# Seven-product pairs for two of four row parts of the feed-forward down projections

## The chip, the core and the metric

The kernel runs on one core of a Trainium2 chip. The time is the device time of one execution in microseconds; several executions are timed and their median is given. One further execution was recorded by the hardware profiler, and all rows of the trace come from it.

## What is computed

The reference is one inference step of a decoder trunk with two layers (DEPTH 2), D_MODEL 1024, 512 prompt tokens and 8 x 4 sample tokens, so 544 token columns in all. Each layer is a half-step feed-forward, a block of three mixers merged by gates, a second half-step feed-forward, and a gated input embedding. Everything is fp32. What the change touches is the feed-forward, with D_FF 2816:

```python
def swiglu(h, w_up, w_down):
    gate, up = jnp.split(h @ w_up, 2, axis=-1)
    return (jax.nn.silu(gate) * up) @ w_down
...
    h = rmsnorm(x, w['g_ffn1'])
    x = x + 0.5 * swiglu(h, w['w_ffn1_up'], w['w_ffn1_down'])
...
    h = rmsnorm(x, w['g_ffn2'])
    x = x + 0.5 * swiglu(h, w['w_ffn2_up'], w['w_ffn2_down'])
```

## The kernel before

Activations lie with channels on the partitions and the 544 tokens on the free axis. Every fp32 value is split into a high part in fp32r (ScalarE copies it) and a low part (VectorE subtracts), and a product is three matmuls: low x high, high x high, high x low.

**Two forms of product.** A plain product (`mm3`, L313) has a 128x128 weight block and runs over 544 columns as two halves of 272, so six matmuls. The seven-product form (`s_pair`, matmuls on L337) takes a pair of output tiles, pairs of input tiles and the two halves of the tokens as a 2x2 by 2x2 block product and does it in seven block products instead of eight, after Winograd. For it the weights W11, W12, W21, W22 are combined into R1 to R4 and the inputs into a *set* per pair of input tiles: B11, B21, B22 and the sums T1 to T4, each of 272 columns with a high and a low part. It keeps four half banks of PSUM, X, Y, Z and V. After the first product ScalarE copies X to Z (L636), after the third it copies X out and VectorE writes V = Y - copy (L640, L641), after the fifth there is one more such pair (L645, L646); the fourth product goes on in Z, the sixth in V, and the third, fifth and seventh in X.

**Weights.** A *unit* is 512 columns of weights: four blocks of a plain product, or the four sets' blocks for one of the seven products. `unit` brings a unit to its end `AHEAD` = 4 units before it is used, in stages: SP loads it (`load`, L234 to L241; for R1 and R2 a POOL DMA adds a second block to what has landed, L242), VectorE adds R3 and R4 (`split_add`, L248), ScalarE makes the high part (`split_hi`, L255), VectorE the low part (`split_lo`, L260). The sums stand two units ahead of the low parts and the loads `LOADS` = 9 units ahead of the sums. All weights and most temporaries live in a pool of 85 slots of 128 x 544; a slot that is given back goes to the end of the queue of free ones, and what is written into it next waits for its last reader.

**A feed-forward.** `ffn` goes over the 22 row tiles of the hidden layer in four row parts of 4, 6, 6 and 6 (`FF_PARTS`). For each tile `ff_group` does the gate and the up projection as one pair, 84 matmuls, whose results are scaled by the norm (L711, L714), put through Silu (L663), multiplied (L666) and split (L669, L672). These closing steps wait in `self.later`: `tick` runs behind each unit, and the step with number n comes n ticks after the pair. The down projection of a part is four pairs of outputs (`down`), all plain in the kernel before: 72 matmuls for six row tiles, 48 for four, and two updates of the residual x (L728). They stand in a queue `todo` and are placed between the pairs of the next part; those of the last part follow at the end. There are four feed-forwards. In each the first tile's projections are plain (four tiles in the first feed-forward).

**Mixing.** `mix` uses seven-product pairs on full sets made by `s_inputs(gain, True)`, for the projections w_in and the gates; plain products there use other operands. TensorE, VectorE, ScalarE, SP and POOL each work through their own instructions in program order.

Of the kernel before, what the change touches and what calls it, by code (L numbers as in the profile page):

```python
# [24 lines left out]
NFF = DFF // P  # L25
FF_PARTS = (4, 6, 6, 6)
NPLE = 2
G = 4
# [9 lines left out]
NSLOT = 85  # L38
LOADS = 9
USE_MERGE = 57  # L40
AHEAD = 4
MAX_AHEAD = 24
# [32 lines left out]
def _places(seq):  # L75
    places = []
    off = 0
    for i, (kind, spec) in enumerate(seq):
        if kind == "P" or spec[0] == 0:
            u0 = i  # L80
            at, off = off, off + P * UC * (1 if kind == "P" else 4)
        places.append((at, u0))
    assert off == N_WEIGHTS
    return places
# [22 lines left out]
class Kern:  # L107
# [99 lines left out]
    def weight(self, u):  # L207
        kind, spec = self.seq[u]
        return (PRODUCTS[spec[0]][0] if kind == "S" else ""), *self.places[u]

    def new_raw(self, w, u0, readers):
        t = self.alloc(F32)
        self.raw[w, u0] = [t, readers]
        return t[0][:, :UC]

    def read_raw(self, w, u0):
        return self.raw[w, u0][0][0][:, :UC]

# [7 lines left out]
    def load(self, u):  # L226
        w, at, u0 = self.weight(u)
        dma = self.nc.sync.dma_start

        def src(i=0, n=1):  # L230
            return self.ins["wts"][at:at + P * UC * n].rearrange("(p c) -> p c", c=UC * n)[:, i * UC:(i + 1) * UC]
# [20 lines left out]
    def split_hi(self, u):  # L252
        w, _, u0 = self.weight(u)
        self.ops[u] = a, b = self.alloc(F32R), self.alloc(F32R)
        self.nc.scalar.activation(a[0][:, :UC], self.read_raw(w, u0), AF.Copy)  # L255

    def split_lo(self, u):
        w, _, u0 = self.weight(u)
        hi, lo = (t[0][:, :UC] for t in self.ops[u])
        self.nc.vector.tensor_sub(lo, self.read_raw(w, u0), hi.bitcast(F32))  # L260
        self.done_raw(w, u0)
# [8 lines left out]
    def unit(self, entry):  # L270
        self.u += 1
        if self.keep:
            self.used += 2
        if self.dry:
            self.seq.append(entry)
            self.use.append(self.used)
            return NULL, NULL
        self.release(self.held)
        to = self.u + AHEAD
        for v in range(self.n_st[3], self.n_st[3] + (self.extra if entry[0] == "P" else 0)):  # L280
            if to < v <= self.u + MAX_AHEAD and self.fits(v + 1):
# [6 lines left out]
        return tuple(t[0][:, :UC] for t in pair)  # L288

# [48 lines left out]

    def s_unit(self, i, name, l, m1, m2):
        assert self.left == 0  # L340
        return self.unit(("S", (i, name, l, m1, m2)))

# [76 lines left out]
    def s_inputs(self, gain, full):  # L419
# [5 lines left out]
        def steps(q):  # L425
# [17 lines left out]
            def hi_b():  # L443
# [13 lines left out]
                tiles.append((b[0][:, :], b[1][:, :]))  # L457
                for src, hi, lo, g in st["b"]:
# [22 lines left out]
            def hi_t():  # L481
                A, B = st["e"][0][0], st["t"][0]
                c = own(*self.rpair())
                if full:
                    d = own(*self.rpair())
                    t1, t4 = ((d[0][:, h], d[1][:, h]) for h in (h1, h2))
                    st["h"] = ((A[:, :], d[0][:, :], d[1][:, :]), (B[:, :], c[0][:, :], c[1][:, :]))
                else:
                    a, d = st["a"], own(self.slot(F32R))
                    t1, t4 = (a[0][:, h2], a[1][:, h2]), (d[0][:, h1], d[1][:, h2])  # L490
                    st["h"] = ((A[:, h1], *t1), (B[:, :], c[0][:, :], c[1][:, :]), (A[:, h2], *t4))
                for src, hi, lo in st["h"]:
                    nc.scalar.activation(hi, src, AF.Copy)  # L493
                sets[q].update(T1=t1, T2=(c[0][:, h1], c[1][:, h1]), T3=(c[0][:, h2], c[1][:, h2]), T4=t4)
# [123 lines left out]

    def s_pair(self, name, l, m1, m2, sets, s1, s2, out):
        nc = self.nc  # L620
        h1, h2 = slice(0, HT), slice(HT, T)
        a, b = s1[0], s2[0]
        banks = [self.ring_bank() for _ in range(4)]
# [4 lines left out]
        for i, (w, x) in enumerate(PRODUCTS):  # L628
            bk = bank[w]
            wt = self.s_unit(i, name, l, m1, m2)  # L630
            new = w in ("W21", "R2")
            for q, xs in enumerate(sets):
                self.mm_s(bk, wt, xs[x], q, new and q == 0, q == len(sets) - 1, not new)
            if w == "W21":
                self.touch(banks[2], sets[0]["B11"][0])
                nc.scalar.activation(Z, X, AF.Copy)  # L636
            elif w == "R2":
                self.touch(banks[3], sets[0]["B11"][0])
            elif w == "R3":
                nc.scalar.activation(a[:, h2], X, AF.Copy)  # L640
                nc.vector.tensor_sub(V, Y, a[:, h2])  # L641
            elif w == "W22":
                out(b, h1, Z)
            elif w == "R1":
                nc.scalar.activation(b[:, h2], X, AF.Copy)  # L645
                nc.vector.tensor_sub(a[:, h2], Y, b[:, h2])  # L646
            elif w == "W12":
                out(a, h1, V)
            elif w == "R4":
                out(b, h2, X)  # L650
            self.tick()

    def ff_group(self, up, l, j, inp, first, plain, hs, hsl):
        nc = self.nc
        t_, o_ = self.slot(), self.slot()
        t, o = t_[0], o_[0]
        a, b = self.rpair()
        hi, lo = a[0][:, :], b[0][:, :]
        hs.append((hi, lo))
        hsl.extend((a, b))  # L660

# [16 lines left out]
        def dr():  # L678
            nc.vector.tensor_mul(o[:, :], o[:, :], self.rstd[:, :])

        if plain > 0:
# [20 lines left out]
            elif plain > 1:  # L702
                fin = (e0, e1, dz, None, d1, d2, d3)
            else:
# [3 lines left out]
        else:  # L708
            r = self.rstd
            self.s_pair(up, l, NFF + j, j, inp.sets, o_, t_,  # L710
                        lambda to, h, ps: nc.vector.tensor_mul(to[:, h], ps, r[:, h]))  # L711

            def dr2():
                nc.vector.tensor_mul(o[:, HT:], o[:, HT:], r[:, HT:])  # L714

            fin = (dz, dr2, d1, d2, d3)
        self.later += [(1 + i, f) for i, f in enumerate(fin) if f]

    def ffn(self, l, which, inp, nxt, tail=None):
        nc = self.nc  # L720
        up, dn = f"w_ffn{which}_up", f"w_ffn{which}_down"
        plain = N_PLAIN if self.start else 1

        def down(m, hs, hsl, j0, last=False):
# [12 lines left out]
        j0 = 0  # L737
        for n in FF_PARTS:
            hs, hsl = [], []
            items = len(todo)  # L740
            for i in range(n):
                j = j0 + i
                self.extra = EXTRA[0] if j < plain else EXTRA[7]
                if j == plain:
                    self.drop(*inp.zs)
                self.ff_group(up, l, j, inp, j == 0, plain - j, hs, hsl)
                while len(todo) > items * (n - 1 - i) // n:
# [38 lines left out]
    def mix(self, l, inp, nxt):  # L786
# [4 lines left out]
        full = self.s_inputs(inp.gain, True)  # L791
        sets, xr, sl = full.sets, full.tiles, full.sl
        steps = self.skew(full.fs, 0, 3) + self.skew(full.fs, 3, 6)
# [4 lines left out]
        def pair(z1, z2, f=None):  # L798
            s1, s2 = self.slot(), self.slot()
            self.s_pair("w_in", l, z1, z2, sets, s1, s2,  # L800
                        lambda to, h, ps: nc.scalar.activation(to[:, h], ps, f or AF.Copy))  # L801
            if f:
# [514 lines left out]
def _layout(inputs, seq):  # L1317
# [9 lines left out]
    for kind, spec in seq:  # L1327
        if kind == "P":
            part = [block(*s) for s in spec]
        elif spec[0] == 0:  # L1330
            _, name, l, m1, m2 = spec
            part = [block(name, l, 2 * q + i, m) for m in (m1, m2) for i in range(2) for q in range(KD // 2)]
        else:
            continue
# [61 lines left out]
```

## Time and profile before

| what | before |
|---|---|
| median of 3 runs | 2403.72 us (2402.2 to 2403.86) |
| profiled execution | 2402.33 us |
| its span, first to last instruction | 2400.6 us |
| TensorE busy | 2386.3 us |
| VectorE busy | 1776.0 us |
| ScalarE busy | 1234.2 us |
| DMA, mean | 137 GB/s |
| mean granted clock of TensorE | 0.999 |

Busy time is the time in which at least one instruction of the engine runs. Matmuls are pipelined and overlap, so that a mean record of 288 ns doesn't mean 288 ns per matmul: the distance between starts is what counts, and it comes from the chain of waits. The profiled execution's own time is 1.7 us longer than its span.

### The profile page before, as it was taken

The numbers are of one execution on the slowest core, as the hardware profiler recorded it, in microseconds if no ns is written. First come the engines' busy times: TensorE is split into PE (matmuls) and PEld (weight loads), VectorE is DVE, ScalarE is ACT, GpSimd is POOL, SyncE is SP. The second block draws the span as 40 slices with busy tenths as digits, with TensorE's granted clock in tenths as the row PEclk, the third lists the DMA queues.
The fourth block names the chain that finished last, engine by engine and source line by source line (L and its number), as shares of the span: only waits on it lengthen the run. The fifth ranks groups of instructions, "written<-read, shape, count | busy, mean of one in ns | idle before, by whom it ended". The sixth has DMA issues, their size and how long they took to land.

```text
span 2400.6 us, 47687 instructions
## 1 busy us (share of the span) xinstructions
PE 2386.3 (99%) x18777; PEld 2371.8 (99%) x18777; DVE 1776.0 (74%) x3212; ACT 1234.2 (51%) x2421; POOL 225.8 (9%) x277
## 2 busy tenths in 40 slices
PE   9999999999999999999999999999999999999998
PEld 9999999999999999999999999999999999999998
DVE  8776667877878777667777766778778777766685
ACT  7544444755565544445554444556556555544463
POOL 1101000111100110100010110001111011101000
PEclk9999999999999999999999999999999999999999
DMA  6655561766554555655165555516555545556431
GB/s 212 143 147 143 145 171 36 178 150 151 149 141 119 145 146 145 150 134 166 55 151 134 144 157 128 167 56 171 146 152 152 150 102 149 152 131 154 128 107 38
DMA packets 180033, 329.76 MB, mean 137 GB/s; under 512 B 20256, under 2 KB 22560, under 8 KB 179808
## 3 DMA queue, kind: packets, MB, share of 16 engines
q1 hardware_dynamic: 141264, 255.92, 34.8%
q0 software_dynamic: 36672, 68.51, 16.9%
q8 instruction: 147, 2.41, 0.4%
q10 hardware_dynamic: 1872, 2.29, 0.3%
q14 instruction: 78, 0.64, 0.1%
HBM read 323.64 MB, written 2.99 MB: 136 GB/s over the span
## 4 chain that ended last, share of the span: by engine, by line
PE 92%; DVE 4%; ACT 3%; issue 0%; DMA 0%; DVEq 0%; ACTq 0%; SPq 0%
PE ps L337 54%; PE ps L313 33%; PE ps L904 2%; PE ps L1170 2%; ACT s L459 1%; DVE s L260 1%; DVE s L498 1%; ACT s L437 1%; DVE acc L400 0%; PE ps L1053 0%; DVE s L469 0%; ACT s L493 0%; ACT s L255 0%; ACT s L399 0%; DVE s L476 0%
## 5 line engine op out<-in xcount | busy, mean ns | idle before, releaser
L337 PE MATMUL ps<-s,s 128*128 128x272 f32 x10332 | 1311.9, 288 | 2.2 <-DVE s L695 2.2
L337 PEld LDWEIGHTS ps<-s,s 128*128 128x128 f32 x10332 | 1302.3, 188 | 3.4 <-DVE s L695 2.8
L313 PE MATMUL ps<-s,s 128*128 128x272 f32 x7536 | 958.9, 288 | 1.3 <-ACT s L459 1.3
L313 PEld LDWEIGHTS ps<-s,s 128*128 128x128 f32 x7536 | 949.8, 188 | 1.6 <-ACT s L459 1.5
L260 DVE TENSOR_TENSOR s<-s,s 128x512 fp32r<-128x512 f32 x1211 | 810.1, 685 | 34.3 <-ACT s L255 32.2
L255 ACT ACTIVATE s<-s 128x512 fp32r<-128x512 f32 x1211 | 710.3, 623 | 188.3 <-DVE s L248 180.3
L242 POOL DMA_DIRECT2D s<-in_wts x246 | 211.0, 872 | 1936.4 <-DMA s<-in_wts 567.3
L636 ACT ACTIVATE ps<-ps 128x272 f32<-128x272 f32 x123 | 47.1, 383 | 493.7 <-PE ps L337 440.1
L728 DVE SCALAR_TENSOR_TENSOR x<-ps,x 128x544 f32<-128x544 f32 x128 | 92.6, 724 | 214.1 <-PE ps L313 213.7
L248 DVE TENSOR_TENSOR s<-s,s 128x512 f32<-128x512 f32 x246 | 168.6, 685 | 0.0
L641 DVE TENSOR_TENSOR ps<-ps,s 128x272 f32<-128x272 f32 x123 | 55.2, 449 | 120.3 <-ACT s L640 119.9
L711 DVE TENSOR_TENSOR s<-ps,rstd 128x272 f32<-128x272 f32 x243 | 106.2, 437 | 11.5 <-PE ps L337 9.9
L640 ACT ACTIVATE s<-ps 128x272 f32<-128x272 f32 x123 | 48.9, 398 | 102.3 <-PE ps L337 101.9
L646 DVE TENSOR_TENSOR s<-ps,s 128x272 f32<-128x272 f32 x123 | 54.3, 441 | 60.1 <-ACT s L645 58.9
L645 ACT ACTIVATE s<-ps 128x272 f32<-128x272 f32 x123 | 48.6, 395 | 66.6 <-PE ps L337 66.4
L801 ACT ACTIVATE s<-ps 128x272 f32<-128x272 f32 x126 | 49.9, 396 | 52.0 <-PE ps L337 51.6
L946 DVE TENSOR_TENSOR s<-ps,s 128x544 f32<-128x544 f32 x48 | 34.8, 725 | 54.6 <-PE ps L313 54.5
L669 ACT ACTIVATE s<-s 128x544 fp32r<-128x544 f32 x88 | 57.9, 658 | 29.0 <-DVE s L666 29.0
L672 DVE TENSOR_TENSOR s<-s,s 128x544 fp32r<-128x544 f32 x88 | 63.3, 720 | 3.6 <-ACT s L669 3.6
L666 DVE TENSOR_TENSOR s<-s,s 128x544 f32<-128x544 f32 x88 | 63.2, 718 | 1.5 <-ACT s L663 1.5
L663 ACT ACTIVATE s<-s 128x544 f32<-128x544 f32 x88 | 57.2, 651 | 11.4 <-DVE s L711 9.7
L1170 PE MATMUL ps<-s,s 128*128 128x256 f32 (+1 forms) x480 | 60.7, 288 | 0.0
(155 smaller groups left out, 1036.7 us busy)
## 6 DMA issues: line engine op xcount, KB each, us to landing
s<-in_wts SPq DMA_DIRECT2D x965, 256.0 KB, 3.3
s<-in_wts POOLq DMA_DIRECT2D x246, 256.0 KB, 5.0
x<-in_xT SPq DMA_DIRECT2D x4, 272.0 KB, 4.5
x<-in_xT ACTq DMA_DIRECT2D x4, 272.0 KB, 5.0
s<-in_pT POOLq DMA_DIRECT2D x4, 272.0 KB, 4.3
out_yT<-s SPq DMA_DIRECT2D x4, 144.0 KB, 1.9
out_yT<-s ACTq DMA_DIRECT2D x4, 144.0 KB, 1.9
s<-in_st_in POOLq DMA_DIRECT2D x2, 272.0 KB, 3.0
```

The costliest lines, as they stand in the source:

```text
L242: self.nc.gpsimd.dma_start(out=t, in_=src(1 if w == "R1" else 2, 4), accum_op=ALU.add)
L248: self.nc.vector.tensor_add(self.new_raw(w, u0, 2 if w == "R3" else 1), self.read_raw(a, u0), self.read_raw(b, u0))
L255: self.nc.scalar.activation(a[0][:, :UC], self.read_raw(w, u0), AF.Copy)
L260: self.nc.vector.tensor_sub(lo, self.read_raw(w, u0), hi.bitcast(F32))
L313: self.nc.tensor.matmul(ps[:, h, :HT], a, bh, start=first and i == 0, stop=last and i == 2)
L337: self.nc.tensor.matmul(ps, a, b, start=first and i == 0, stop=last and i == 2, skip_group_check=go_on)
L666: nc.vector.tensor_mul(o[:, :], o[:, :], t[:, :])
L669: nc.scalar.activation(hi, o[:, :], AF.Copy)
L672: nc.vector.tensor_sub(lo, o[:, :], hi.bitcast(F32))
L711: lambda to, h, ps: nc.vector.tensor_mul(to[:, h], ps, r[:, h]))
L728: nc.vector.scalar_tensor_tensor(xm, self.pv(pst[i]), 0.5, xm, op0=ALU.mult, op1=ALU.add)
L1170: nc.tensor.matmul(ps, a, b[:, c], start=first and i == 0, stop=last and i == 2)
```

## The change

The down projections of row parts 1 and 2 of every feed-forward (`FF_S`) run as seven-product pairs (`down_fast`), three sets for six row tiles, so that a unit of their weights has 384 columns instead of 512. The sets are made in `ff_group` out of two gated tiles: the steps e1 (even tile) and e2 and t (odd tile) take the place of the plain split d2 and d3. The pair's results go to x in quarter steps of 272 columns. The four pairs of such a part run two behind the first and two behind the second gate pair of the next part (`DRAIN`). `unit`'s loads are 7 instead of 9 units ahead of the sums, the low parts 5 instead of 4 ahead of the use. In the mixing sets the second half of the first tile's split is no longer made (nothing reads it), and T1 takes its place, so that a set has seven slots instead of eight. In the first feed-forward the closing steps from d1 on come some ticks later.

```diff
+DRAIN = 2, 2, 0, 0, 0, 0
+FF_S = (False, True, True, False)
...
-LOADS = 9
+LOADS = 7
...
-AHEAD = 4
+AHEAD = 5
...
+    def width(self, u):
+        kind, spec = self.seq[u]
+        return UC if kind == "P" else P * spec[-1]
...
                 if full:
-                    st["b"] = [(E1[:, :], a[0][:, :], a[1][:, :], g1)]
-                    tiles.append((a[0][:, :], a[1][:, :]))
+                    st["b"] = [(E1[:, h1], a[0][:, h1], a[1][:, h1], g1)]
...
-                if full:
-                    d = own(*self.rpair())
-                    t1, t4 = ((d[0][:, h], d[1][:, h]) for h in (h1, h2))
-                    st["h"] = ((A[:, :], d[0][:, :], d[1][:, :]), (B[:, :], c[0][:, :], c[1][:, :]))
-                else:
-                    a, d = st["a"], own(self.slot(F32R))
-                    t1, t4 = (a[0][:, h2], a[1][:, h2]), (d[0][:, h1], d[1][:, h2])
-                    st["h"] = ((A[:, h1], *t1), (B[:, :], c[0][:, :], c[1][:, :]), (A[:, h2], *t4))
+                a, d = st["a"], own(self.slot(F32R))
+                t1, t4 = (a[0][:, h2], a[1][:, h2]), (d[0][:, h1], d[1][:, h2])
+                st["h"] = ((A[:, h1], *t1), (B[:, :], c[0][:, :], c[1][:, :]), (A[:, h2], *t4))
...
+        def e1_hi():
+            self.drop(t_)
+            st.update(a=self.rpair(), o=o_)
+            hsl.extend(st["a"])
+            nc.scalar.activation(st["a"][0][0][:, h1], o[:, h1], AF.Copy)
+
+        def e1_lo():
+            a = [p[0] for p in st["a"]]
+            nc.vector.tensor_sub(a[1][:, h1], o[:, h1], a[0][:, h1].bitcast(F32))
+
+        def e2_hi():
+            st["b"] = self.rpair()
+            hsl.extend(st["b"])
+            nc.scalar.activation(st["b"][0][0][:, :], o[:, :], AF.Copy)
+            A, B = st["o"][0], t
+            nc.vector.tensor_sub(B[:, h2], A[:, h2], o[:, h2])
+            nc.vector.tensor_sub(B[:, h1], B[:, h2], A[:, h1])
+
+        def e2_lo():
+            b, A, B = [p[0] for p in st["b"]], st["o"][0], t
+            nc.vector.tensor_sub(A[:, h1], A[:, h1], A[:, h2])
+            nc.vector.tensor_add(A[:, h2], o[:, h1], B[:, h1])
+            nc.vector.tensor_sub(b[1][:, :], o[:, :], b[0][:, :].bitcast(F32))
+            self.drop(o_)
+
+        def t_hi():
+            c, d = self.rpair(), self.slot(F32R)
+            hsl.extend((*c, d))
+            A, B = st["o"][0], t
+            a, b, c, d = *([p[0] for p in st[k]] for k in "ab"), [p[0] for p in c], d[0]
+            st["h"] = ((A[:, h1], a[0][:, h2], a[1][:, h2]), (B[:, :], c[0][:, :], c[1][:, :]), (A[:, h2], d[:, h1], d[:, h2]))
+            for src, hi, _ in st["h"]:
+                nc.scalar.activation(hi, src, AF.Copy)
...
+        def t_lo():
+            for src, hi, lo in st["h"]:
+                nc.vector.tensor_sub(lo, src, hi.bitcast(F32))
+            self.drop(st["o"], t_)
...
-                fin = (e0, e1, dz, None, d1, d2, d3)
+                fin = (e0, e1, dz) + (None,) * 4 + (d1, None, d2, d3)
...
-            fin = (dz, dr2, d1, d2, d3)
+            fin = (dz, dr2, d1) + ((d2, d3) if not fast else (e1_hi, e1_lo) if j % 2 == 0 else (e2_hi, e2_lo, t_hi, t_lo))
...
+        def down_fast(m, hs, hsl, j0):
+            t_ = self.slot()
+            a2, b2 = t_[0][:, HT:], t_[0][:, :HT]
+
+            def add(i, h, src):
+                x = self.x[m + i][:, h]
+                nc.vector.scalar_tensor_tensor(x, src, 0.5, x, op0=ALU.mult, op1=ALU.add)
+
+            self.s_pair(dn, l, m, m + 1, hs, a2, b2, add, j0 // 2)
+            add(0, slice(HT, T), a2)
+            self.drop(t_)
+            if m == KD - 2:
+                self.drop(*hsl)
...
+                self.ff_group(up, l, j, inp, j == 0, plain - j, hs, hsl, fast, st)
+                if part and FF_S[part - 1]:
+                    for _ in range(min(DRAIN[i], len(todo))):
+                        down_fast(*todo.popleft())
                 while len(todo) > items * (n - 1 - i) // n:
                     down(*todo.popleft())
```

## Rows read from the trace of the kernel before

**Rows 1.** Page, busy times: us, share of the span, instructions.

```profile
PE 2386.3 (99%) x18777; PEld 2371.8 (99%) x18777; DVE 1776.0 (74%) x3212; ACT 1234.2 (51%) x2421; POOL 225.8 (9%) x277
```

**Rows 2.** Waits of TensorE: who waited for whom, us in total, times, longest.

```profile
PE ps L337 <- DVE s L695: 2.2, 3, 0.7
PE ps L313 <- ACT s L459: 1.3, 1, 1.3
```

**Rows 3.** Chain that ended last, 100 to 300 us: start us, us, what.

```profile
153.88 9.03 PE ps L313 x72
162.92 10.51 PE ps L337 x84
```

**Rows 4.** Groups of TensorE by form: shapes, count, busy us, mean ns, idle before.

```profile
L337 PE MATMUL ps<-s,s 128*128 128x272 f32 x10332 | 1311.9, 288 | 2.2 <-DVE s L695 2.2
L313 PE MATMUL ps<-s,s 128*128 128x272 f32 x7536 | 958.9, 288 | 1.3 <-ACT s L459 1.3
...
L616 PE MATMUL ps<-s,ones_r 128*128 128x272 f32 x7 | 2.0, 287 | 0.0
```

**Rows 5.** One row part, two pairs: us, busy (count) of PE, PEld, DVE, ACT, POOL; clock, DMA, GB/s.

```profile
132.84:232.15 99.31, 99.31 (x794) 99.31 (x794) 68.37 (x123) 42.86 (x84) 10.24 (x12) 1.00 0.58 143
...
182.46:203.60 21.14, 21.14 (x170) 21.14 (x170) 16.96 (x32) 11.02 (x22) 3.02 (x4) 1.00 0.66 167
```

**Rows 6.** Groups of VectorE by form, whole run: busy us, mean ns.

```profile
L260 DVE TENSOR_TENSOR s<-s,s 128x512 fp32r<-128x512 f32 x1211 | 810.1, 685 | 34.3 <-ACT s L255 32.2
...
L711 DVE TENSOR_TENSOR s<-ps,rstd 128x272 f32<-128x272 f32 x243 | 106.2, 437 | 11.5 <-PE ps L337 9.9
...
L672 DVE TENSOR_TENSOR s<-s,s 128x544 fp32r<-128x544 f32 x88 | 63.3, 720 | 3.6 <-ACT s L669 3.6
...
L641 DVE TENSOR_TENSOR ps<-ps,s 128x272 f32<-128x272 f32 x123 | 55.2, 449 | 120.3 <-ACT s L640 119.9
```

**Rows 7.** Timeline of VectorE, 150 to 200 us: start us, us, what.

```profile
185.00 0.72 DVE L672 TENSOR_TENSOR s<-s,s 128x544 fp32r<-128x544 f32 x1
185.64 0.68 DVE L260 TENSOR_TENSOR s<-s,s 128x512 fp32r<-128x512 f32 x1
...
188.43 0.69 DVE L248 TENSOR_TENSOR s<-s,s 128x512 f32<-128x512 f32 x1
189.03 0.43 DVE L711 TENSOR_TENSOR s<-ps,rstd 128x272 f32<-128x272 f32 x1
189.38 0.68 DVE L260 TENSOR_TENSOR s<-s,s 128x512 fp32r<-128x512 f32 x1
```

**Rows 8.** Timeline of VectorE in the output projection, 1930 to 1940 us.

```profile
1930.25 0.44 DVE L476 TENSOR_TENSOR s<-s,s 128x272 f32<-128x272 f32 x1
1930.72 0.44 DVE L477 TENSOR_TENSOR s<-s 128x272 f32<-128x272 f32 x1
1931.20 0.44 DVE L478 TENSOR_TENSOR s<-s,s 128x272 f32<-128x272 f32 x1
```

**Rows 9.** Windows in the merge stage of the second layer: us, busy by engine.

```profile
1810.00:1820.00 10.00, 10.00 (x82) 10.00 (x82) 9.58 (x20) 5.83 (x16) 0.00 (x0) 1.00 0.38 133
1840.00:1850.00 10.00, 10.00 (x82) 10.00 (x81) 9.50 (x21) 4.95 (x14) 2.13 (x3) 1.00 0.58 144
```

**Rows 10.** Timeline of ScalarE, 182 to 204 us.

```profile
187.04 0.40 ACT L640 ACTIVATE s<-ps 128x272 f32<-128x272 f32 x1 [1.04 <-PE ps L337]
187.33 0.62 ACT L255 ACTIVATE s<-s 128x512 fp32r<-128x512 f32 x1
...
190.40 1.66 ACT L255 ACTIVATE s<-s 128x512 fp32r<-128x512 f32 x3
```

**Rows 11.** Page, DMA issues: KB each, median us to landing.

```profile
s<-in_wts SPq DMA_DIRECT2D x965, 256.0 KB, 3.3
s<-in_wts POOLq DMA_DIRECT2D x246, 256.0 KB, 5.0
```

**Rows 12.** The weight tensor's transfers, SP's and POOL's together.

```profile
DMA to landing us min/median/max: 2.4/3.6/7.8
```

More of the change, by code (lines that the diff above doesn't have):

```diff
@@ L213, in new_raw @@
         self.raw[w, u0] = [t, readers]
-        return t[0][:, :UC]
+        return t[0][:, :self.width(u0)]
     def read_raw(self, w, u0):
-        return self.raw[w, u0][0][0][:, :UC]
+        return self.raw[w, u0][0][0][:, :self.width(u0)]
     def done_raw(self, w, u0):
@@ L228, in load @@
         dma = self.nc.sync.dma_start
+        c = self.width(u)
         def src(i=0, n=1):
-            return self.ins["wts"][at:at + P * UC * n].rearrange("(p c) -> p c", c=UC * n)[:, i * UC:(i + 1) * UC]
+            return self.ins["wts"][at:at + P * c * n].rearrange("(p c) -> p c", c=c * n)[:, i * c:(i + 1) * c]
         if w == "":
@@ L254, in split_hi @@
         self.ops[u] = a, b = self.alloc(F32R), self.alloc(F32R)
-        self.nc.scalar.activation(a[0][:, :UC], self.read_raw(w, u0), AF.Copy)
+        self.nc.scalar.activation(a[0][:, :self.width(u)], self.read_raw(w, u0), AF.Copy)
     def split_lo(self, u):
         w, _, u0 = self.weight(u)
-        hi, lo = (t[0][:, :UC] for t in self.ops[u])
+        hi, lo = (t[0][:, :self.width(u)] for t in self.ops[u])
         self.nc.vector.tensor_sub(lo, self.read_raw(w, u0), hi.bitcast(F32))
@@ L287, in unit @@
         self.held = () if self.keep else pair
-        return tuple(t[0][:, :UC] for t in pair)
+        return tuple(t[0][:, :self.width(self.u)] for t in pair)
     def fits(self, v):
@@ L456, in hi_b @@
                 st["b"].append((E2[:, :], b[0][:, :], b[1][:, :], g2))
-                tiles.append((b[0][:, :], b[1][:, :]))
+                if not full:
+                    tiles.append((b[0][:, :], b[1][:, :]))
                 for src, hi, lo, g in st["b"]:
@@ L617, in touch, with s_pair @@
             self.written.add(bank[1])
-    def s_pair(self, name, l, m1, m2, sets, s1, s2, out):
+    def s_pair(self, name, l, m1, m2, sets, a2, b2, out, k0=0):
         nc = self.nc
         h1, h2 = slice(0, HT), slice(HT, T)
-        a, b = s1[0], s2[0]
         banks = [self.ring_bank() for _ in range(4)]
@@ L629, in s_pair @@
             bk = bank[w]
-            wt = self.s_unit(i, name, l, m1, m2)
+            wt = self.s_unit(i, name, l, m1, m2, k0, len(sets))
             new = w in ("W21", "R2")
@@ L639, in s_pair, with ff_group @@
             elif w == "R3":
-                nc.scalar.activation(a[:, h2], X, AF.Copy)
-                nc.vector.tensor_sub(V, Y, a[:, h2])
+                nc.scalar.activation(a2, X, AF.Copy)
+                nc.vector.tensor_sub(V, Y, a2)
             elif w == "W22":
-                out(b, h1, Z)
+                out(1, h1, Z)
             elif w == "R1":
-                nc.scalar.activation(b[:, h2], X, AF.Copy)
-                nc.vector.tensor_sub(a[:, h2], Y, b[:, h2])
+                nc.scalar.activation(b2, X, AF.Copy)
+                nc.vector.tensor_sub(a2, Y, b2)
             elif w == "W12":
-                out(a, h1, V)
+                out(0, h1, V)
             elif w == "R4":
-                out(b, h2, X)
+                out(1, h2, X)
             self.tick()
-    def ff_group(self, up, l, j, inp, first, plain, hs, hsl):
+    def ff_group(self, up, l, j, inp, first, plain, hs, hsl, fast, st):
         nc = self.nc
@@ L656, in ff_group @@
         t, o = t_[0], o_[0]
[L657 to L660, printed above, removed]
+        h1, h2 = slice(0, HT), slice(HT, T)
+        if not fast:
+            a, b = self.rpair()
+            hi, lo = a[0][:, :], b[0][:, :]
+            hs.append((hi, lo))
+            hsl.extend((a, b))
         def dz():
@@ L737, in ffn @@
         j0 = 0
-        for n in FF_PARTS:
-            hs, hsl = [], []
+        for part, n in enumerate(FF_PARTS):
+            hs, hsl, st = [], [], {}
+            fast = FF_S[part]
             items = len(todo)
@@ L791, in mix @@
         full = self.s_inputs(inp.gain, True)
-        sets, xr, sl = full.sets, full.tiles, full.sl
+        sets, sl = full.sets, full.sl
         steps = self.skew(full.fs, 0, 3) + self.skew(full.fs, 3, 6)
@@ L799, in pair @@
             s1, s2 = self.slot(), self.slot()
-            self.s_pair("w_in", l, z1, z2, sets, s1, s2,
-                        lambda to, h, ps: nc.scalar.activation(to[:, h], ps, f or AF.Copy))
+            self.s_pair("w_in", l, z1, z2, sets, s1[0][:, HT:], s2[0][:, HT:],
+                        lambda i, h, ps: nc.scalar.activation((s1, s2)[i][0][:, h], ps, f or AF.Copy))
             if f:
@@ L1330, in _layout @@
         elif spec[0] == 0:
-            _, name, l, m1, m2 = spec
-            part = [block(name, l, 2 * q + i, m) for m in (m1, m2) for i in range(2) for q in range(KD // 2)]
+            _, name, l, m1, m2, k0, n = spec
+            part = [block(name, l, 2 * q + i, m) for m in (m1, m2) for i in range(2) for q in range(k0, k0 + n)]
         else:
```

14 lines of the change are left out of this document (8 added, 6 removed).

## Prediction

> **What bounds the kernel now.** I read the page's busy times first, then who made TensorE wait, then the chain of waits, and only then the other engines. TensorE is busy for 2386.3 of 2400.6 us [rows 1]. All its waits for another engine's result come to a few microseconds, and the longest entry is 2.2 us in three places [rows 2]. The chain of waits, from 153 to 173 us, is nothing but matmuls: 72 in 9.03 us, then 84 in 10.51 us [rows 3], both 0.125 us per matmul. So time is the number of 272-column matmuls times 0.125 us, as long as the engines that prepare operands keep ahead; the groups of the page count 10332 of them in seven-product pairs and 7536 in plain products [rows 4]. What the reader is to see next is how near VectorE is to being the limit: in one row part of six pairs and four plain down pairs it is busy for 68.37 of 99.31 us, in a stretch of two pairs alone for 16.96 of 21.14 us [rows 5].
>
> **TensorE's sum.** A plain down pair over six row tiles is 2 outputs x 6 x 3 products x 2 halves = 72 matmuls. The seven-product form on three sets is 7 x 3 x 3 = 63. That removes 9 x 0.1253 = 1.13 us, and a pair takes 7.89 instead of 9.02 us. Two parts x four pairs x four feed-forwards = 32 pairs, so 36.1 us go. The filling matmuls that a pair issues on a bank that the ring has not written yet ran 7 times in the whole kernel before [rows 4]; a pair that follows a pair finds its banks written, so I count none more. The profiled execution took 2402.3 us, so without any new wait it would be 2366.2 us.
>
> **VectorE's price of an instruction.** The mean record is 685 ns for 512 columns, 720 for 544, 437 to 449 for 272 [rows 6]. But in a full queue the next instruction starts before the record of the last has ended: a 512-column one 0.60 us later, a 272-column one 0.35 us later, a 544-column one 0.64 us later [rows 7]. I use these pitches. For 384 columns, which the trace doesn't show, the bounds are 0.35 and 0.60; the line between the 272 and 544 pitches gives 0.47, taken. Where each instruction reads what the last has written, the pitch of 272 columns is about 0.48 [rows 8]; the new sums on the activations are such a sequence.
> The Trainium skill (VectorE: DVE Perf Modes, "The DRAIN you can't avoid") says that the next operation doesn't start until the pipeline of the one before has emptied, though it lets one that is not held start earlier. By the rule a row of 512 would cost its whole 0.685 us, by the trace 0.60; the trace decides here, and what the rule would make of the time is the second rival below.
>
> **What VectorE gains and loses.** A plain down pair costs it three low splits and two updates of x, 3 x 0.60 + 2 x 0.64 = 3.08 us. The new pair has seven low splits and two weight sums of 384 columns (9 x 0.47 = 4.23), two PSUM subtractions (0.70) and four 272-column updates of x (1.44): 6.37 us within 7.89 us of TensorE. In a fast part the activations' split changes too. For two row tiles it was 2 x 0.64 = 1.28 us; now it is 0.35 for the first half-tile's low part, 0.83 for two dependent sums, 1.47 for two more and a 544 low part, and 1.34 for the three low parts of the sums: 3.99, so 2.71 more per two tiles, 8.1 per part.
> From the measured part [rows 5]: part 1 (fast, its downs still plain over four tiles, so one low split fewer in each) is 68.4 - 2.4 + 8.1 = 74.1 of 6 x 10.52 + 4 x 6.02 = 87.2 us. Part 2 (fast, with fast downs) is 68.4 - 12.3 + 25.5 + 8.1 = 89.7 of 6 x 10.52 + 4 x 7.89 = 94.7 us, 95%. Part 3 is 81.5 of 94.7. In the merge stage of before, two stretches of 10 us have VectorE busy for 9.58 and 9.50 us while TensorE has no gap [rows 9]. So the average still fits, and only bunching can cost.
>
> **Where it bunches.** The down pairs run two by two behind the first and second gate pair of the next part. The closing steps of a gate pair come one per product of what follows. Behind the second gate pair of part 2 they are the heavy ones (0.35 + 0.64 + 0.83 + 1.47 + 1.34 = 4.6 us) and fall into one 7.89 us down pair beside its own 6.37: 11.0 in 7.9. Adding up VectorE's queue in program order, it is full from the third product on, and the weight sum for the last product, issued at 6.8 us of the pair, ends at about 10.5. ScalarE's split of that block waits for it, and the copy of the first product is queued behind the split. In a full queue a 512-column split takes 0.52 to 0.55 us and a 272-column copy 0.29 [rows 10], so I take 0.42 for a split of 384 columns and 0.30 for the copy; they end near 11.3. TensorE wants that copy at 10.14, before the third product: a wait of 1.2 us, and 0.1 more for the PSUM difference before the sixth product. That is 1.3 us per feed-forward.
> The second place is the start of the down pairs of each fast part. The last low parts of the sets are issued behind the last product of the gate pair in front. By the same addition the set that the second product needs is ready at about 13.1 us, and TensorE is there at 12.65: 0.5 us, twice per feed-forward. Together 2.3 us x 4 = 9.2 us, with bounds of 0 (if ready instructions wait less than I add) and twice that.
>
> **What I cost at nothing.** ScalarE gains 4 x (7 x 0.42 + 3 x 0.30 - 3 x 0.55) = 8.8 us in a part and some 3 us for the sets; its 42.9 of 99.3 us [rows 5] become about 55 of 94.7. If that cover went, each of its late copies would cost what I put on the place above. Weight loads rise from 768 to 1344 KB per down pair; in part 2 that is 6 x 1792 + 4 x 1344 KB in 94.7 us, 174 GB/s against 143, so the DMA share of 0.58 [rows 5] becomes about 0.71. The mixing sets split half a tile less and use one slot fewer per pair of tiles: a few tenths of a microsecond of VectorE and ScalarE, eight times, behind the plain gemm and the value product, where TensorE has no waits. AHEAD 5 moves one more weight split in front of the first group; ScalarE does that under the first group's 96 matmuls (12 us). The later steps of the first plain groups only move VectorE's work to a later product. Two loads less in flight are taken up with the last rival.
>
> **The rivals.** First, no new waits: 2366 in the profiled run. For it speaks that TensorE waits nowhere in all the pairs of before [rows 2]; against it the bunching just added up, which before has nowhere.
> Second, VectorE becomes the bound of part 2, at full record length: a gate pair costs 9 x 0.685 + 0.449 + 0.441 + 4 x 0.437 + 2 x 0.72 = 10.2, with the sets 11.8; a down pair with 0.55 for 384 columns is 7.7. Part 2 is then 6 x 11.8 + 4 x 7.7 = 101.6 against 94.7 us, 6.9 too much, four times 27.6: about 2394. Against it: two pairs at 10.2 would be 20.4 us busy, where the row has 16.96 [rows 5].
> This is the time by the Trainium skill's rule named above; the starts 0.60 us apart [rows 7] speak against it.
> Third, slower: a weight sum waits for its raw weights. A raw block is loaded on SP's queue and then added to by a POOL DMA, 3.3 and 5.0 us to landing in the median, up to 7.8 for one [rows 11, 12]: 8.3 us together, less for 192 KB. The sum on VectorE stood nine products behind the load and now stands seven: 7 x 1.503 = 10.5 us in gate pairs, which covers it, but 7 x 1.127 = 7.9 us in down pairs. VectorE can be about two products (2.25 us) late before TensorE waits. There are 16 runs of two down pairs; each would have to lose 36.1 / 16 = 2.26 us to eat the saving, so it decides from a chain of 7.9 + 2.25 + 2.26 = 12.4 us on. With 13 us the time is 2366 + 16 x 2.9 = 2412. Queued behind such a sum are VectorE's PSUM readers, for which TensorE waits. The operands of fast parts take 7 slots per two tiles instead of 4, so loads may have to wait for slots, which speaks for it; the medians speak against it.
>
> **How the numbers follow.** Forecast 2366.2 + 9.2 = 2375.4 against the profiled 2402.3; the median of the runs is 1.4 us above that run, so 2376.8, rounded to 2376. The chances: this one 0.52 (own range 2369 to 2385), no waits 0.22, VectorE the bound 0.15, late weights 0.08, something between that leaves no difference 0.03. The range 2364 to 2395 holds the first three and leaves out some 0.13. Within 0.2% (4.8 us, about what a measurement can tell from no change) is 2399 to 2409: 0.05. Faster 0.87, slower 0.08.
>
> **What would show it.** Right: 288 fewer matmuls overall, seven-product ones up by 32 x 63 = 2016; matmul pitch still 0.125 us; TensorE idle before the pair products for 5 to 15 us in total, released by VectorE or ScalarE, at the start of down pairs and in the third product of the fourth down pair of a part 2; VectorE near 9.5 tenths there. Wrong: down pairs that take over 9 us throughout, VectorE waiting for DMA at its weight sums, or idle SP queues that wait for slots of the down pairs.

## The result

The changed kernel takes 2384.56 us in the median (2383.55 to 2384.96, 4 runs) against 2403.04; the ratio is 0.9922, with a 95% interval of 0.9905 to 0.9940. It is 18.5 us faster; the forecast was 2376, with a range of 2364 to 2395. The profiled execution took 2383.55 us with a span of 2381.8. So of the 36.1 us that the matmuls were to bring, about half arrived.

Busy times, and TensorE's groups by form, after the change, against [rows 1, 4] (in the rows DVE is VectorE, ACT ScalarE, and PEld TensorE's weight loads):

```profile
PE 2358.7 (99%) x18489; PEld 2337.9 (98%) x18489; DVE 1931.5 (81%) x3708; ACT 1341.3 (56%) x2725; POOL 281.1 (12%) x341
```

```profile
L344 PE MATMUL ps<-s,s 128*128 128x272 f32 x12348 | 1568.8, 288 | 11.0 <-ACT ps L637 6.3 <-DVE s L723 3.7 <-DVE s L740 0.7
L320 PE MATMUL ps<-s,s 128*128 128x272 f32 x5232 | 665.1, 288 | 1.5 <-ACT s L466 1.5
...
L618 PE MATMUL ps<-s,ones_r 128*128 128x272 f32 x7 | 2.0, 288 | 0.0
```

The counts are those of the sum: 2016 more in pairs, 2304 fewer plain, 288 fewer in all, and the filling matmuls stay at 7. VectorE rose from 1776 to 1931.5 us. The waits of TensorE and then of its weight loads (who waited for whom, us in total, times, longest), against [rows 2]:

```profile
PE ps L344 <- ACT ps L637: 6.3, 5, 1.4
PE ps L344 <- DVE s L723: 3.7, 8, 0.5
PE ps L320 <- ACT s L466: 1.5, 1, 1.5
...
PE ps L344 <- DVE s L740: 0.7, 1, 0.7
```

```profile
PEld ps L344 <- ACT ps L637: 9.5, 15, 1.6
PEld ps L344 <- DVE s L723: 5.4, 8, 0.7
```

L637 is ScalarE's copy of the first product, L723 the low parts of the sums (`t_lo`): the two forecast places, 4 times 1.4 us and 8 times 0.46 us. The fifth wait for L637, 0.64 us at 59.6 us, is in the first seven-product pair of the first feed-forward; the kernel before has none there. But these idle times are too small. A matmul's record is 288 ns long at a pitch of 125, so the first 0.16 us of each wait lies under a record; a weight load's is 188, and the same eight waits are 5.4 us there and not 3.7.

The distance between two pairs says it without that error. Part 2 holds the four down pairs of part 1 and part 3 those of part 2; the fourth of part 2 is the one behind the heavy steps, called the heavy place below. ScalarE's copy of the third product (L641) starts as soon as TensorE is done with it unless ScalarE is late. These are its starts in the second feed-forward of layer 0, from the first gate pair of part 2 to the third (in square brackets, the idle time before it and what ended it):

```profile
903.70 0.40 ACT L641 ACTIVATE s<-ps 128x272 f32<-128x272 f32 x1 [1.25 <-PE ps L344]
...
913.90 0.40 ACT L641 ACTIVATE s<-ps 128x272 f32<-128x272 f32 x1 [0.77 <-PE ps L344]
...
921.91 0.40 ACT L641 ACTIVATE s<-ps 128x272 f32<-128x272 f32 x1 [0.48 <-PE ps L344]
...
930.93 0.40 ACT L641 ACTIVATE s<-ps 128x272 f32<-128x272 f32 x1 [1.76 <-PE ps L344]
...
940.35 0.40 ACT L641 ACTIVATE s<-ps 128x272 f32<-128x272 f32 x1 [0.49 <-PE ps L344]
...
950.19 0.38 ACT L641 ACTIVATE s<-ps 128x272 f32<-128x272 f32 x1
...
959.20 0.40 ACT L641 ACTIVATE s<-ps 128x272 f32<-128x272 f32 x1 [1.00 <-PE ps L344]
```

By the matmul counts at 0.1253 us the distances would be 9.40 (gate pair to down pair), 7.89 (down to down) and 9.02 (down to gate). They are 10.20, 8.01, 9.02, 9.42, 9.84, 9.01. What is over is the loss of that place. The mean over the four feed-forwards, in us:

| from ... to the third product of | part 2 | part 3 |
|---|---|---|
| first gate pair to first down pair | 0.80 | 0.75 |
| first to second down pair | 0.13 | 0.64 |
| third to fourth down pair | 1.95 | 0.26 |
| all others together | 0.37 | 0.19 |

That is 5.1 us per feed-forward, 20.4 in all. Against the 2366.2 us without waits the profiled run has lost 17.4. Some 2 of the 3 us between the two lie outside parts 2 and 3: from the first gate pair of part 2 to the last of part 3 the four feed-forwards take 735.7 us against 752.5, and all else takes 1646.1 against 1648.1.

In the first down pair of a part 2 and at the heavy place (the fourth) VectorE has no gap to speak of (0.04 us), in part 2 as a whole it has. Columns: stretch, its length, busy time and count of TensorE, its weight loads, VectorE, ScalarE, POOL, then clock, DMA share, GB/s. The first row is part 2, the second its first down pair, the third the fourth.

```profile
898.97:997.05 98.08, 96.23 (x758) 95.21 (x757) 86.39 (x183) 56.34 (x121) 17.12 (x20) 1.00 0.69 168
909.49:918.00 8.51, 8.05 (x64) 7.80 (x63) 8.51 (x21) 5.36 (x13) 1.71 (x2) 1.00 0.77 200
944.63:954.47 9.84, 8.45 (x65) 8.05 (x64) 9.80 (x22) 6.46 (x14) 0.85 (x1) 1.00 0.47 138
```

The timelines of VectorE and of ScalarE at that place show the chain that was forecast: the last weight sum (L255) ends in VectorE's full queue, ScalarE's split (L262) waited 1.21 us for it, and the copy of the first product (L637) stands behind the split.

```profile
946.16 0.43 DVE L775 SCALAR_TENSOR_TENSOR x<-ps,x 128x272 f32<-128x272 f32 x1
946.51 0.55 DVE L267 TENSOR_TENSOR s<-s,s 128x384 fp32r<-128x384 f32 x1
946.98 0.55 DVE L255 TENSOR_TENSOR s<-s,s 128x384 f32<-128x384 f32 x1
947.45 0.43 DVE L775 SCALAR_TENSOR_TENSOR x<-ps,x 128x272 f32<-128x272 f32 x1
947.80 1.42 DVE L723 TENSOR_TENSOR s<-s,s 128x272 fp32r<-128x272 f32 x3
```

```profile
947.62 0.52 ACT L262 ACTIVATE s<-s 128x384 fp32r<-128x384 f32 x1 [1.21 <-DVE s L255]
948.05 0.38 ACT L637 ACTIVATE ps<-ps 128x272 f32<-128x272 f32 x1
```

By the starts of its matmuls TensorE loses 1.66 us there before the third product, where the prediction had 1.2, and 0.2 before the sixth, where it had 0.1.

One thing is new: VectorE waits for raw weights, which it did nowhere before.

```profile
DVE s L255 <- DMA s<-in_wts: 17.0, 16, 2.3
```

### The profile page after: what moved, and what is told of

The parts are those of the page before. It is cut to its first block, busy times and chain, and to the rows that moved or that the text cites. A ratio compares the mean times of both kernels' runs of the same rounds, so it can differ in the third digit from the quotient of the medians.

```text
span 2381.8 us, 48122 instructions
## 1 busy us (share of the span) xinstructions
PE 2358.7 (99%) x18489; PEld 2337.9 (98%) x18489; DVE 1931.5 (81%) x3708; ACT 1341.3 (56%) x2725; POOL 281.1 (12%) x341
## 5 line engine op out<-in xcount | busy, mean ns | idle before, releaser
L344 PE MATMUL ps<-s,s 128*128 128x272 f32 x12348 | 1568.8, 288 | 11.0 <-ACT ps L637 6.3
L344 PEld LDWEIGHTS ps<-s,s 128*128 128x128 f32 x12348 | 1555.7, 188 | 19.0 <-ACT ps L637 9.5
L262 ACT ACTIVATE s<-s 128x512 fp32r<-128x512 f32 (+1 forms) x1339 | 770.9, 604 | 309.0 <-DVE s L255 289.9
L267 DVE TENSOR_TENSOR s<-s,s 128x512 fp32r<-128x512 f32 (+1 forms) x1339 | 854.5, 661 | 50.3 <-ACT s L262 49.4
L320 PE MATMUL ps<-s,s 128*128 128x272 f32 x5232 | 665.1, 288 | 1.5 <-ACT s L466 1.5
L320 PEld LDWEIGHTS ps<-s,s 128*128 128x128 f32 x5232 | 659.1, 188 | 1.8 <-ACT s L466 1.7
L249 POOL DMA_DIRECT2D s<-in_wts x310 | 265.5, 881 | 1858.0 <-DMA s<-in_wts 564.4
L255 DVE TENSOR_TENSOR s<-s,s 128x512 f32<-128x512 f32 (+1 forms) x310 | 203.6, 657 | 17.2 <-DMA s<-in_wts 17.0
L642 DVE TENSOR_TENSOR ps<-ps,s 128x272 f32<-128x272 f32 x155 | 69.3, 447 | 93.9 <-ACT s L641 93.9
L637 ACT ACTIVATE ps<-ps 128x272 f32<-128x272 f32 x155 | 59.2, 382 | 146.8 <-PE ps L344 118.0
L641 ACT ACTIVATE s<-ps 128x272 f32<-128x272 f32 x155 | 61.5, 396 | 136.9 <-PE ps L344 136.8
L646 ACT ACTIVATE s<-ps 128x272 f32<-128x272 f32 x155 | 60.9, 393 | 69.6 <-PE ps L344 69.5
L787 DVE SCALAR_TENSOR_TENSOR x<-ps,x 128x544 f32<-128x544 f32 x64 | 46.0, 722 | 50.3 <-PE ps L320 50.0
L864 ACT ACTIVATE s<-ps 128x272 f32<-128x272 f32 x126 | 49.8, 395 | 49.4 <-PE ps L344 48.8
L1233 PEld LDWEIGHTS ps<-s,s 128*128 128x128 f32 x480 | 60.4, 188 | 0.0
L967 PE MATMUL ps<-s,s 128*128 128x512 f32 x240 | 55.8, 393 | 0.0
```

Of the source, the lines that this page charges most:

```text
L255: self.nc.vector.tensor_add(self.new_raw(w, u0, 2 if w == "R3" else 1), self.read_raw(a, u0), self.read_raw(b, u0))
L262: self.nc.scalar.activation(a[0][:, :self.width(u)], self.read_raw(w, u0), AF.Copy)
L320: self.nc.tensor.matmul(ps[:, h, :HT], a, bh, start=first and i == 0, stop=last and i == 2)
L344: self.nc.tensor.matmul(ps, a, b, start=first and i == 0, stop=last and i == 2, skip_group_check=go_on)
L641: nc.scalar.activation(a2, X, AF.Copy)
L642: nc.vector.tensor_sub(V, Y, a2)
```

## The experiments

The theory after the result: TensorE loses time where VectorE's queue is late around the down pairs, through whatever it happens to wait for. Rivals: late weights; a fixed loss in each down pair; a few unlucky places in program order that an edit of order removes. Times are medians against 2402.3 to 2402.7 us of the kernel before on the same chips; all edits are on the changed kernel. "Losses" are the distances over the count, as above.

**1. Down pairs away from the heavy steps.**

```diff
-DRAIN = 2, 2, 0, 0, 0, 0
+DRAIN = 2, 0, 2, 0, 0, 0
```

> Edit: the second two down pairs of a fast part run behind the third gate pair of the next part instead of the second (DRAIN = 2, 0, 2, 0, 0, 0). The second gate pair closes with the heavy steps of an odd tile (4.6 us of VectorE), the third with the light ones of an even tile. Theory (VectorE's queue is full where the heavy steps and a down pair meet): TensorE's wait for ScalarE's copy of the first product, 6.3 us in all, goes, and as much again that hides inside matmul records near it; 2376 to 2379 us against the 2384.6 of the change. Rival, late weights: the loads stand as close as before, so 2384 or more. Rival, a fixed loss in every down pair: 2384.

2386.0 us, ratio 0.9931 (0.9918 to 0.9944): a miss. The 1.95 us fell to some 1.0 (0.36 and 0.63 in the second feed-forward), but VectorE's waits for raw weights doubled, and one gate pair behind them lost 0.6 to 2.3 us in each feed-forward.

```profile
DVE s L255 <- DMA s<-in_wts: 34.8, 27, 2.9
```

**2. Loads earlier.**

```diff
-LOADS = 7
+LOADS = 9
```

> Edit: loads 9 instead of 7 units ahead of the weight sums, all else as in the change. In the change VectorE waits 17.0 us in 16 places for a raw weight block before a weight sum. Theory (VectorE's queue): that wait goes to near 0, but only the part of it that reaches TensorE comes back, some 0.8 us per feed-forward behind the second two down pairs of part 1: 2380 to 2382 us. Rival, late weights are the main loss: 2370 us or less. Rival, slots: the pool of 85 runs short, loads wait for slots anyway and nothing changes: 2384.

2385.0 us, a miss: the wait for weights is gone, and the time is the same, so in the change as it is late weights are not where the time goes: the loss per feed-forward goes from 5.1 to 4.9 us only. The slots' rival gave this time, but not for this reason, since the loads no longer come late.

```profile
DVE s L255 <- DMA s<-in_wts: 2.8, 3, 1.4
```

The small gain is given back elsewhere: all that lies outside parts 2 and 3 takes 1648.2 us, as in the kernel before. In part that is the wait of a feed-forward's first pair for the plain products' scaling (L740), 0.7 us in one place with 7, which comes back in three places (1.5 us), where it was before the change [rows 2].

**3. Operands four units ahead.**

```diff
-AHEAD = 5
+AHEAD = 4
```

> Edit: operands 4 instead of 5 units ahead of their use, loads still 7 ahead of the sums. With 5, the sum for the seventh product of a pair falls into the seventh unit of the pair in front and ScalarE's split of it stands in front of the copy of the first product; with 4 it stands behind that copy. Theory: the 6.3 us wait for that copy goes, but low parts are only four units (4.5 us in down pairs) ahead while VectorE is up to 4.4 us late, so new small waits for low parts: 2377 to 2385 us. Rival, late weights: same lead, no change, 2384. Rival, a longer lead is what makes the pairs run: 2390 us or more.

2404.6 us (its profiled run 2401.0): the whole gain is gone, and the theory's number was far off. The losses are 8.1 us per feed-forward, 3.26 at the heavy place and 1.31 in a gate pair that had none. TensorE now waits for the copy of the third product.

```profile
PE ps L344 <- ACT s L641: 8.1, 8, 1.8
```

By program order that fits: with 4 the seventh product's sum stands behind `t_lo` too, later in the same full queue, and its split in front of the copy of the third product instead of the first. This step is argued, not shown by itself. The rest of the time lies outside the two parts and in the difference between median and profiled run.

**4. No fast part.**

```diff
-FF_S = (False, True, True, False)
+FF_S = (False, False, False, False)
```

> Edit: no part of the down projection runs as seven-product pairs (FF_S all False); the mixing sets without the unused half, AHEAD 5 and LOADS 7 stay. Theory: all of the gain is the 288 matmuls, the rest costs and gives nothing: 2401 to 2404 us. Rival, the rest gives something of its own (the profiles differ by up to 2 us outside the changed parts): 2399 to 2401. Rival, the shorter load lead costs everywhere: above 2405.

2401.2 us, ratio 0.9995 (0.9986 to 1.0004). All that can be told from no change comes from the down pairs; the mixing sets and the constants are worth about 1 us, which the interval doesn't tell from nothing.

**5. No low parts of the sums.** T1 to T4 use their high part twice, and `t_lo` subtracts nothing, so this kernel doesn't compute the reference.

```diff
         def t_lo():
-            for src, hi, lo in st["h"]:
-                nc.vector.tensor_sub(lo, src, hi.bitcast(F32))
```

> Leaves out the low parts of the four sums T1 to T4 in the fast parts' sets: the three subtractions of t_lo are not made, and the products use the high part twice, so TensorE runs the same 18489 matmuls. VectorE has 1.34 us less per odd tile, 4.0 us per fast part. Theory (TensorE waits because VectorE's queue is late around the down pairs): the waits at the start of the down pairs (8 times 0.75 us) go, the one behind the heavy steps (4 times 1.95 us) goes for the most part; 2370 to 2376 us. Rival, a fixed loss in each down pair on TensorE or ScalarE: 2384. Rival, late weights: 2383 to 2385.

2379.1 us, ratio 0.9899 (0.9884 to 0.9914), a gain short of the 2370 to 2376 expected. With the same matmuls, 5.5 us come back from VectorE's work alone. The first down pairs lose 0.18 instead of 0.80 and 0.75; here the third products of the first gate pair of a part 2, of the first down pair and of the second:

```profile
902.98 0.40 ACT L641 ACTIVATE s<-ps 128x272 f32<-128x272 f32 x1 [1.25 <-PE ps L344]
...
912.56 0.40 ACT L641 ACTIVATE s<-ps 128x272 f32<-128x272 f32 x1 [0.15 <-PE ps L344]
...
920.47 0.40 ACT L641 ACTIVATE s<-ps 128x272 f32<-128x272 f32 x1 [0.74 <-PE ps L344]
```

The low parts that the first down pairs waited for don't exist in this kernel, but the second down pairs of part 3, which didn't wait for them, fall too, from 0.64 to 0.23. Late weights take some back: VectorE's waits for them rise from 17.0 to 26.4 us, and one second down pair loses 1.54 us behind the longest of those in a down pair. The heavy place only falls from 1.95 to 1.69: the weight sum that it hangs on stands in front of `t_lo` in the queue, which I had overlooked in the expectation.

**6. T2 and T3 first.**

```diff
-            st["h"] = ((A[:, h1], a[0][:, h2], a[1][:, h2]), (B[:, :], c[0][:, :], c[1][:, :]), (A[:, h2], d[:, h1], d[:, h2]))
+            st["h"] = ((B[:, :], c[0][:, :], c[1][:, :]), (A[:, h1], a[0][:, h2], a[1][:, h2]), (A[:, h2], d[:, h1], d[:, h2]))
```

> Edit: the sums T2 and T3 (one tile) are split before T1 and T4 instead of behind T1; nothing else. The second product of a down pair reads T3, the fifth T1. Theory: the low part of T3 ends one 272-column subtraction (0.35 us) earlier, so the 3.7 us in 8 waits for L723 fall to about 1 us and the time by 2 to 3 us: 2381.5 to 2382.5. Rival, that wait is for something else or the time is lost a product later: 2384.

2384.9 us: the rival. The first down pairs lose 0.35 less, as worked out, and the second ones 0.35 more. The weight loads' waits moved from L723 to the copy of the fifth product:

```profile
PEld ps L344 <- ACT s L646: 4.0, 8, 0.6
PEld ps L344 <- DVE s L723: 2.6, 8, 0.3
```

This is the clearest single reading: in these pairs what TensorE waits for is only the first thing that VectorE's lateness meets.

**7. Operands six units ahead.**

```diff
-AHEAD = 5
+AHEAD = 6
```

> Edit: operands 6 instead of 5 units ahead, loads still 7 ahead of the sums. With 4 the excess at the heavy steps was 3.25 us per feed-forward, with 5 it was 1.95. With 6 the weight sum of the seventh product stands in the sixth unit of the pair in front, one low split, one reader and one sum earlier in VectorE's queue, some 0.8 to 1.3 us. Theory: that excess falls to 0.5 to 1.0, 4 to 6 us in all, less what slots cost: 2378 to 2381. Rival, the pool of slots is too small for it and loads come late: 2384 or more. Rival, units ahead don't matter in themselves: 2384.

2408.9 us, ratio 1.0026 (1.0016 to 1.0036): slower than the kernel before, with 11.7 us lost per feed-forward in its profiled run (2414.0 us). Waits for raw weights are 35.2 us, as the slots' rival has it, and TensorE waits for the copy of the third product in 25 places, also where no weight is late, as at each heavy place, where 3.64 us are lost.

```profile
PE ps L344 <- ACT s L641: 21.5, 25, 2.4
```

Which of the two weighs more wasn't taken apart. Of 4, 5 and 6, only 5 keeps the gain.

**8. Edits 1 and 2 together.**

> Edit: both edits of the first two runs, DRAIN = 2, 0, 2, 0, 0, 0 and LOADS = 9. The first alone took 0.9 us per feed-forward off the heavy place but lost 1.7 where VectorE waits for raw weights (34.8 us in 27 places against 17.0); the second alone took those waits to 2.8 us. Theory: together the gain of the first stays, 4 x 0.9 = 3.5 us: 2380 to 2382. Rival, what the two down pairs cost moves with them and is the same anywhere: 2384 to 2386.

2383.5 us (2382.7 to 2384.6), ratio 0.9918 (0.9903 to 0.9933), 1.5 us below run 2 alone. In three of four feed-forwards the losses are 0.6 to 0.9 us smaller than in run 2, in one a late weight takes it back. Less than expected, and not clear of the changed kernel.

**9. ScalarE's split later.**

```diff
-        for i, d in ((3, 0), (2, 1), (1, 2), (0, 2 + LOADS)):
+        for i, d in ((3, 0), (2, 0), (1, 2), (0, 2 + LOADS)):
```

> Edit: ScalarE's high-part split is issued in the same unit as VectorE's low part instead of one unit earlier; AHEAD 5 and LOADS 7 stay. The split of a pair's seventh product then stands behind the copy of the first product of the pair in front of it, not before it, while its weight sum keeps its place in VectorE's queue. Theory (the copy is late because it stands behind a split that waits for VectorE's weight sum): the waits for L637 fall from 6.3 to under 2 us, the second down pairs of each two lose their 0.14 to 0.67 us, and at the heavy steps the wait for the PSUM difference (L642) takes over with about 1.1 of the 1.95 us: 2377 to 2381. Rival, VectorE's lateness costs the same whoever is waited for: 2383 to 2386. Rival, VectorE now waits for ScalarE in every unit: above 2387.

2388.2 us. The waits for L637 fell from 6.3 to 1.5 us, so the chain over the split was read rightly; and the heavy place still loses 2.01 us, with 0.37 more behind it, now spread over four waits, for the copies of the fifth, the first and the third product and for the PSUM difference. So taking one split away from one copy gives nothing, which fits VectorE's lateness as the bound; but the copy of the third product there stands behind another split that waits for VectorE, so that the order on ScalarE is not ruled out by this run. The time is that of the last rival: VectorE waits for ScalarE's splits, 193.1 us against 49.4, all that lies outside parts 2 and 3 takes 1650.8 us instead of 1646.1, and in the mixer pairs go from 10.54 to 10.80 us:

```profile
DVE s L267 <- ACT s L262: 193.1, 249, 4.8
```

**10. Weight sums earlier.**

```diff
-        for i, d in ((3, 0), (2, 1), (1, 2), (0, 2 + LOADS)):
+        for i, d in ((3, 0), (2, 1), (1, 3), (0, 3 + LOADS)):
```

> Edit: VectorE's weight sums are issued one unit earlier (three units ahead of the low parts instead of two), the loads stay seven units ahead of them. The seventh product's sum then stands in the sixth unit of the pair in front. Theory: at the heavy steps it ends 0.8 us earlier, so 1.95 us becomes 1.1 to 1.3, and the second pairs lose most of their excess: 2379 to 2382. Rival, slots (one more raw block is held): loads come late, DMA waits above 30 us, 2385 or more. Rival, VectorE's lateness costs the same: 2384.

2384.5 us (2381.8 to 2386.6): inconclusive in time. The loss per feed-forward falls from 5.1 to 4.3 us, most of it in part 3's second pairs (0.64 to 0.31, 0.26 to 0); the heavy place stays, at 2.07. There the wait for the copy of the first product falls from 1.4 to 0.6 us, and one for the copy of the third, which the changed kernel has nowhere, takes its place:

```profile
PE ps L344 <- ACT s L641: 2.2, 4, 0.5
```

The mixer loses 1.0 to 1.6 us per layer.

**11. One fast part.**

```diff
-FF_S = (False, True, True, False)
+FF_S = (False, True, False, False)
```

> Edit: only row part 1 runs as seven-product down pairs (FF_S = False, True, False, False), 144 matmuls fewer than with none (2401.2 us) and 144 more than the change. The down pairs then run behind gate pairs whose closing steps are the plain ones, so the heavy place does not exist. Theory: the excess is that of the light places alone, 0.75 + 0.67 + 0.25 us per feed-forward as in part 3 of the change: 2401.2 - 18.0 + 6.7 = 2389.9, between 2389 and 2391; twice this gain (22.6 us) is more than the change has (16.6). Rival, every down pair loses the same: half of the change's gain, 2393. Rival, loads: 2393 or more.

2389.0 us (2388.5 to 2389.3), ratio 0.9944 (0.9929 to 0.9959): as worked out from the light places. One part brings 12.2 us of its 18.0; the second brings 4.5 of 18.0. Of the 13.5 us that the second loses, some 7 are the losses of its own down pairs, much like the first one's (1.8 us per feed-forward, the table's column for part 3), and some 6 are the rise in part 2 from 1.8 to 3.2 us per feed-forward, where its heavy closing steps meet the first one's down pairs.

**12. Edits 1, 2 and 10 together**, the last only within feed-forwards.

> Edit: the run with DRAIN = 2, 0, 2, 0, 0, 0 and LOADS = 9 (2383.5 us), and the weight sums one unit earlier as in the run with early sums, but only within the feed-forwards behind row part 0, since in the mixer that edit cost 1.1 to 1.6 us per layer. Early sums took 1.0 to 1.3 us off each feed-forward. Theory: the two add, 2383.5 - 4 x 1.0 = 2379.5, between 2378 and 2381.5, the fastest of all. Rival, slots: with one more raw block the pool runs short and loads are late, 2383 or more. Rival, both edits take the same lateness away once: 2382 to 2383.5.

2384.8 us (2383.3 to 2386.0): a miss, no better than the change. From the third gate pair of part 2 to the third down pair it takes 11.2 us where run 8 takes 9.6, in every feed-forward. TensorE's waits for the copy of the first product (here L638), 0.4 us in run 8, are back:

```profile
PE ps L345 <- ACT ps L638: 7.5, 8, 1.5
```

## Why the prediction was right, and what was mis-sized

The direction, the bound and the mechanism held. The matmul count and its price were exact: 288 fewer, distances of undisturbed pairs still 9.02 and 10.52 us. The pitches held as well: 0.47 us for 384 columns (946.51 to 946.98 above), records of 0.55. The Trainium skill (VectorE: DVE Perf Modes, "The DRAIN you can't avoid") says that the next operation starts only when the pipeline of the one before is empty, unless it is one that is not held; the trace again has it 0.08 us before the end of the record. Part 2, which would have been overfull at full record length, has VectorE busy for 86.4 of 98.1 us (I had 89.7 of 94.7). So the second rival is out (at its own prices a down pair comes to 7.6 and not 7.7 us, which changes nothing). The first is out by the waits above. What spoke for it, that TensorE waits nowhere in the pairs of before, is not quite so: its rows have three waits of 0.7 us, each at the first pair of a feed-forward [rows 2].

The terms that were too small are those of "Where it bunches": 2.3 us per feed-forward, measured 5.1, just above its upper bound of twice that. The start of the down pairs was put at 0.5 us twice and measured 0.80 and 0.75; the heavy place at 1.3, measured 1.95. And I stopped adding once the awaited operand was ready. VectorE stays late behind it, since a down pair needs 6.4 of 7.9 us itself, and so the distances to the second pairs hold 0.13, 0.64 and 0.26 us, which the sum hasn't (half of the 0.64 is lost at the first pair's seventh product, half at the next pair's third); runs 6 and 10 show that this lateness is paid at another instruction if the first is relieved. That VectorE's work is the cause is shown by run 5 for the first and second down pairs, which also rules out a fixed loss in each pair. For the heavy place, where run 5 took away little, it rests on the rows above, in which VectorE is busy for 9.80 of 9.84 us, and on run 1, which moved the down pairs away from the heavy steps and halved the loss. Some 0.5 us per feed-forward lies in gate pairs, part of it where raw weights were late. That the time still came out at the slow end of this forecast's own range (2369 to 2385) is in part luck: the losses exceed the bound, and 2 us came back in stretches where the sum has nothing.

The third rival (late weights) was real as a wait, 17.0 us on VectorE, mostly at gate pairs behind the down pairs (1.8 of the 17.0 in down pairs), but run 2 shows it cost next to nothing in time. It costs time where the down pairs are moved: run 8, which is run 1 with earlier loads, is 2.5 us faster than run 1.

What I had costed at nothing was perhaps worth a little: the mixing sets and constants gave about 1 us (run 4), not clear of nothing. By run 2 it comes with the loads: with 7 in reserve two of three waits of 0.7 us at the start of a feed-forward go, with 9 they are back. The code suggests why, since with fewer loads in reserve plain products may be prepared further ahead. AHEAD 5, which I treated as free, is no free choice: 4 and 6 lose the whole gain. What part of that is the place of the sums in the queues, and what is slots, stays open. The new wait at 59.6 us goes with the 5: run 4, without fast parts, has it, and run 3, with AHEAD 4, has not.

## What to carry to other kernels

When matmuls are traded for vector work on a kernel bound by TensorE, look at the busiest stretch of the vector engine and not at its average: here VectorE was busy for 88% of part 2 (95% in the prediction), and half the gain was lost all the same. Add the queue up product by product, and go on adding until it is empty again, not only to the first late operand. When relieving one wait moves the loss to the next instruction by the same amount, the lateness of the queue is the quantity to cut, as leaving out 1.34 us of it per odd tile did; none of the reorderings tried here brought a time clearly below the changed kernel's.

## What the runs showed that I had not expected

Idle time of TensorE in a profile with overlapping records understates short waits: 3.7 us by its matmuls and 5.4 by its weight loads for the same eight waits, and 6.2 us by the distance between pairs, which also holds what follows each wait (the next matmul starts 0.23 us later instead of 0.125). And the lead of the operands has no single direction: 4, 5 and 6 units ahead gave 2404.6, 2384.6 and 2408.9 us.
